# Loads, halves and norm transposes of a two-layer hybrid decoder trunk: second weight rows in halves, a small early read, later transposes

## The chip, the cores and the metric

The kernel runs on one core of a Trainium2 chip. The metric is the device time of one execution in microseconds (us), lower is better. The engines are named as the profile names them: PE (matmuls; PEld its weight loads), DVE (vector), ACT (scalar), POOL (GpSimd) and SP (which here only issues DMAs). A "q" behind an engine's name (SPq, ACTq) marks its sequencer, where DMAs are issued.

## What is computed

Two layers of a decoder trunk on 256 tokens of 1024 values in float32, with three groups of heads side by side, all of 64 wide: 6 stick-breaking heads (`sb`), 6 block-sparse heads with rotary positions (`mb`; with 256 tokens there is one block, so this is causal softmax attention), and 4 heads that attend to 256 memory tokens (`mem`). Cut from the reference:

```python
for layer in range(DEPTH):
    h = rms_norm(x, norm_g[layer])
    proj = jnp.einsum('btd,dc->btc', h, w_in[layer])
    sb_q, sb_k, sb_v, sb_g, mb_q, mb_k, mb_v, mb_g, mem_q, mem_g = jnp.split(proj, split_at, axis=-1)
    o_sb = stick_breaking_attention(sb_q, sb_k, sb_v) * jax.nn.silu(sb_g)
    o_mb = moba_attention(partial_rotary(mb_q), partial_rotary(mb_k), mb_v) * jax.nn.silu(mb_g)
    mk, mv = jnp.split(rms_norm(mem, mem_norm_g[layer]) @ w_mem_kv[layer], 2, axis=-1)
    o_mem = memory_attention(mem_q, mk, mv) * jax.nn.silu(mem_g)
    x = x + jnp.concatenate([o_sb, o_mb, o_mem], axis=-1) @ w_out[layer]
return rms_norm(x, final_norm_g)
```

`w_in` has 3584 columns in each layer, `w_mem_kv` 512 and `w_out` 1024, each over 1024 rows, that is 8 blocks of 128 rows (k = 0 to 7).

## The kernel before, in words

**Weights.** The columns of the weights are cut into pieces (`sb_qk`, `mem_q`, `mb_k` and so on, class `Piece`) whose order in each layer is the table `ORDER`. A piece is cut into chunks of up to 768 columns in all: 768 columns of one block of rows, or 384 of two, or 256 of three. A chunk is read by one DMA into one of 5 buffers `raw` (`dma_chunk`, the DMA itself in the helper `dma`, L332). Then it is split into two parts, hi = the weights cast to fp32r (`hi_task`; `copy`, L266 on DVE, or `act`, L245 on ACT) and lo = raw - hi (`lo_task`, `tt`, L251, DVE), which stand side by side in one of 7 buffers `hl`. The split of a chunk sets its `raw` free, and `lo_task` then issues the next chunk's DMA. A product is made of three matmuls: hi by hi, hi by the activations' lo, and lo by the activations' hi (`mm`, L229). The very first chunk of `sb_qk` (k = 0) is read as two halves of 384 columns; all others come whole.

**Activations.** The first layer's input comes transposed from HBM (`xT`) into the tile `uT`, in blocks of 128 rows: `load_xT`. The norm gain is multiplied in block by block, ACT making the hi part (`scale_hi`, L247) and DVE the lo part (`scale_lo`, L255) of the tile `T`. The first piece runs over k on the outside with six PSUM banks open, so that PE can begin when block 0 of weights and of x is there; for k = 0 it works on the two halves one after the other (`groups` in `main`), for k = 1 to 3 on all six column groups at once, first hi, then lo. At the change of layer `norm_task` multiplies the rows by gain and 1/rms (`stt`, L255, tile `w`, 512 columns at a time), PE transposes four blocks (`tr`, L234), and ACT and DVE copy the bank out as hi and lo into `T`: four such groups, two row halves by two column halves.

**Order of the work.** The program is written out by a scheduler in Python, `Sched`. Every task is a generator that asks for an engine, names what it needs and which buffers it takes, and has a priority; `run` takes the task whose modelled start (`_avail`) is earliest, within a small slack by priority, and `op` adds a modelled cost to the engine's clock. `main` holds the matmuls of the projections, with the lowest priority; scores, sums, turns, norm transposes are tasks of their own and are put between them. What decides is modelled times, so a constant changes the order on all engines. `X67_AT`, `X0_AT`, `X1_AT` and `CST_AT` say behind which chunk's DMA the loads of x blocks 6 and 7, of the rows of x and of the constants are issued; `TRIP_LAT` is the modelled time of a trip through DRAM (`trip`).

In softmax heads (`soft_head`) the four buffers `w` (also used by the norm) are handed out in a fixed order of head pairs: the `mb` pairs first, then the `mem` pairs, by this condition:

```python
first = (2 if mb else 0) if MEM_FIRST[l] else (0 if mb else 3)
_, (w,) = yield R("act", alloc=["w"], cond=lambda: 5 * l + first + h // 2 <= turn["w"] + 1)
```

**Queues at the start.** ACT's queue issues the two halves of k = 0 and then the x block of k = 1; SP's queue issues `gc` (gain columns), x block 0, the chunk of k = 1, x block 2, the chunk of k = 2, x block 3, the chunk of k = 3, and x blocks 4 and 5 together. POOL sets the constant tile `negone` (a memset, L452) and issues one broadcast of the norm's gain row later (`bcast_row`, L447). Score stages and the products with the values work on 64 rows or 64 columns of the PE array (`pair_scores`, `pair_task`), and the scheduler holds them back so as to run them in blocks (`_by_form`).

Of the kernel before, what the change touches and what calls it, by code (L numbers as in the profile page):

```python
# [17 lines left out]
KT = 8  # L18
# [10 lines left out]
KORD = (0, 1, 2, 3, 4, 5, 6, 7)  # L29
LAT_SAME, LAT_CROSS = 130.0, 240.0  # L30
P_H0 = -8
P_RX = 1
# [3 lines left out]
URG = 2  # L36
X67_AT = 6
CST_AT = 7
X0_AT = 9
X1_AT = 12  # L40
DMA_GBS = 380.0
SP_ISSUE = 450.0
DMA_LAT = 2200.0
DMA_GBS_1K = 300.0
TRIP_LAT = 4000.0
MEM_FIRST = (False, False)
MEM_AT = 1
ORDER = (["sb_qk", "mem_q", "mb_k", "mb_q", "mk", "mv", "sb_v", "sb_g", "mb_g", "mb_v", "mem_g"],
         ["mk", "mv", "sb_g", "mb_k", "mb_q", "mb_g", "mem_g", "sb_q", "mem_q", "sb_k", "sb_v", "mb_v"])
GATES = {"sb_g": ((0, 1, 2),), "mb_g": ((0, 1, 2),), "mem_g": ((0,), (1,))}  # L50
HOLD = 4000.0
SPARE2 = 2
DVE_HI = 400.0
# [27 lines left out]
class Sched:  # L81
# [37 lines left out]
    def _avail(self, k, eng):  # L119
        r = k.req  # L120
        t = k.t
# [17 lines left out]
        if cond is not None and not cond():  # L139
            return None  # L140
        return t

# [56 lines left out]
def hybrid_trunk(ctx: ExitStack, tc: tile.TileContext, x, mem, norm_g, w_in, w_mem_kv, w_out,  # L199
# [171 lines left out]
    for p in order:  # L371
        i = 0
        while i < KT:
            kk = [p.kord[i]]
            i += 1
            while i < KT and len(kk) < p.nk and p.kord[i] == kk[-1] + 1:
                kk.append(p.kord[i])
                i += 1
            half = p.width // 2 if not chunks else p.width
            for c in range(0, p.width, half):  # L380
                for n, k in enumerate(kk):
                    p.kmap.setdefault(k, []).append((c, len(chunks), n * half))
                chunks.append((p, kk, c, half))
# [20 lines left out]
    def hi_task():  # L404
        for j, (p, kk, _, w) in enumerate(chunks):
            w = len(kk) * w
            e, _ = yield R(*([] if j == 0 else [("act", 0.833 * w)]), ("dve", 0.52 * w + DVE_HI), 
                           need=[("raw", j)] + ([("free", j - LEAD)] if j >= LEAD else []))
            copy(his[j % LEAD][:, :w], raws[j % RAW][:, :w], e)
            S.mark(("hi", j))  # L410
            prog["hi"] = j + 1
# [18 lines left out]
    def load_xT(k0, k1, q=None, now=0.0):  # L430
        dma(uT[:, k0:k1, :], xT_r[:, k0:k1, :], ("xT", k0), q, now)
        for k in range(k0 + 1, k1):
            S.ready["xT", k] = S.ready["xT", k0]

    dma(gc, gcols, "gc")
    dma_chunk(q=nc.scalar)
    load_xT(0, 1)
    dma_chunk(q=nc.scalar)
    load_xT(1, 2, nc.scalar)
    for k in range(2, 4):  # L440
        dma_chunk()
        load_xT(k, k + 1)
    dma_chunk()
    load_xT(4, 6)

# [124 lines left out]
    def norm_task(l, t, H, done):  # L570
# [3 lines left out]
        for q in range(2):  # L574
            s = slice(q * 512, (q + 1) * 512)
            _, (w,) = yield R("dve", need=[("gb", 0)], alloc=["w"])
            stt(w, src[:, s], r, gb[:, s], OP.mult, OP.mult)
            _, (pt,) = yield R("pe", alloc=["bank"])
            for i in range(4):
# [36 lines left out]
    wTs, scs, sps, ws, Fs, ropes = {}, {}, {}, {}, {}, {}  # L616
    turn = {"sb": 0, "w": 0}
    HCOL = {"sb": 0, "mb": 384, "mem": 768}
# [16 lines left out]
    def pair_scores(l, kind, c):  # L635
# [20 lines left out]
        if kind != "mem":  # L656
            yield R("pe")
            for h in range(2):
                for j, o in enumerate((slice(0, 128), slice(256, 384))):
                    if kind == "sb":  # L660
                        mm(sc[h][:, o], masks[:, 0, :], identb, False, j == 1)
                    else:
                        mm(sc[h][:, o], identb, masks[:, 1, :], False, j == 1)
        for h in range(2):
            S.mark(("qkdone", l, kind, 2 * c + h))
            scs[l, kind, 2 * c + h] = sc[h]
# [42 lines left out]
    def soft_head(l, h, kind):  # L709
        mb = kind == "mb"  # L710
        first = (2 if mb else 0) if MEM_FIRST[l] else (0 if mb else 3)
        reg = [(0, 128), (128, 384)] if mb else [(0, 256), (256, 512)]
        _, (st,) = yield R("dve", alloc=["st"], need=[("qkdone", l, kind, h)])
        sc = scs.pop((l, kind, h))
        for t, (r0, r1) in enumerate(reg):
            nc.vector.tensor_reduce(st[:, t:t + 1], sc[:, r0:r1], axis=AX.X, op=OP.max, negate=True)  # L716
            S.op("dve", 1.0417 * (r1 - r0) + 65.0)
            if t == 0:
                yield R("dve")
        _, (w,) = yield R("act", alloc=["w"], cond=lambda: 5 * l + first + h // 2 <= turn["w"] + 1)  # L720
        for t, (r0, r1) in enumerate(reg):
# [255 lines left out]
    def main():  # L977
# [26 lines left out]
        for l in range(DEPTH):  # L1004
# [45 lines left out]
            if l == 0:  # L1050
# [4 lines left out]
                for k in range(KT):  # L1055
                    if k < 4:
                        groups = [range(3), range(3, 6)] if k == 0 else [range(6)]
                        for g in groups:
# [131 lines left out]
```

## Time and profile before

| | |
|---|---|
| median of 3 runs | 282.25 us (281.93 to 282.3) |
| the profiled execution's own time | 281.82 us |
| its span in the profile | 280.0 us |
| mean granted clock of PE in it | 0.998 of full speed |
| busy: PE, DVE, ACT, POOL | 270.7, 229.9, 185.0, 3.9 us |
| moved by DMA | 60.49 MB, mean 216 GB/s |

The span runs from the first to the last recorded instruction; the execution's own time is 1.8 us longer. Busy times are sums over the engine's instructions, so PE at 97% has some 9 us in which it does nothing; the share says nothing of where these lie. The list of waits of an engine says what ended each stand; the timeline gives start, duration and the stand before it in square brackets.

### The profile page before, as it was taken

To read this page: it belongs to the slowest core of one execution; us is meant where nothing else is said; L and a number is where in the kernel's file an instruction comes from. 1 tells how busy PE (TensorE), PEld (TensorE's weight loads), DVE (VectorE), ACT (ScalarE), POOL (GpSimd) and SP (SyncE) were. 2 spreads that over 40 slices of the span, in tenths; PEclk is the share of its full clock that TensorE was granted. 3 is DMA by queue.
4 is the path that set the end of the run, shared out by engine and by line. 5 is a ranking of instruction groups with operands and counts; after the bars stand their busy time and mean duration, and the time that the engine had idled before them with its cause. 6 is when DMAs were issued, how large, how long until landed. Compare 5 with 4: busy or idle time off the path is not lost.

```text
span 280.0 us, 4979 instructions
## 1 busy us (share of the span) xinstructions
PE 270.7 (97%) x1713; PEld 242.7 (87%) x1713; DVE 229.9 (82%) x514; ACT 185.0 (66%) x414; POOL 3.9 (1%) x10
## 2 busy tenths in 40 slices
PE   7899999999999999999999999999999999999991
PEld 4788999898888898898978899988888898988991
DVE  3789899998999999995889489739999999994273
ACT  3879799984696787771866384648974898433053
POOL 0030000010000000000000000000000000000000
PEclk9999999999999999999999999999999999999999
DMA  6999938697588998885476846857358988890004
GB/s 218 348 385 367 367 103 259 188 246 285 165 267 212 263 314 250 242 210 167 129 248 199 272 147 208 250 167 218 104 148 290 248 265 219 263 248 14 0 0 150
DMA packets 45720, 60.49 MB, mean 216 GB/s; under 512 B 3328, under 2 KB 42368, under 8 KB 45696
## 3 DMA queue, kind: packets, MB, share of 16 engines
q1 hardware_dynamic: 44688, 58.22, 67.7%
q0 software_dynamic: 288, 1.05, 1.5%
q10 hardware_dynamic: 720, 0.92, 1.0%
q8 instruction: 13, 0.21, 0.3%
q14 instruction: 11, 0.09, 0.1%
HBM read 53.89 MB, written 6.29 MB: 215 GB/s over the span
## 4 chain that ended last, share of the span: by engine, by line
PE 91%; DMA 4%; ACT 2%; DVE 2%; issue 1%; ACTq 0%; DVEq 0%
PE bank L229 90%; DMA uT<-xT_dram 2%; DMA raw<-in_w_in_dram 2%; PE bank L234 1%; DVE hl L251 1%; ACT hl L245 1%; DVE xs L251 0%; ACT junk L247 0%; DVE w L255 0%; ACT rn L247 0%; ACT ss L247 0%; ACT T L247 0%; ACT T L245 0%; ACTq L332 0%; ACT L206 0%
## 5 line engine op out<-in xcount | busy, mean ns | idle before, releaser
L251 DVE TENSOR_TENSOR hl<-raw,hl 128x768 fp32r<-128x768 f32 (+2 forms) x111 | 101.2, 919 | 8.8 <-ACT hl L245 7.3
L229 PE MATMUL bank<-T,hl 128*128 128x512 f32 (+1 forms) x582 | 106.6, 340 | 1.6 <-ACT hl L245 1.1
L229 PEld LDWEIGHTS bank<-T,hl 128*128 128x128 f32 x582 | 89.2, 190 | 15.7 <-ACT hl L245 1.3
L245 ACT CAST hl<-raw 128x768 fp32r<-128x768 f32 (+2 forms) x100 | 79.4, 808 | 21.2 <-PE bank L229 16.1
L229 PE MATMUL bank<-hl,T 128*128 128x384 f32 (+1 forms) x448 | 82.0, 337 | 0.0
L229 PEld LDWEIGHTS bank<-hl,T 128*128 128x128 f32 x448 | 76.4, 188 | 1.6 <-issue 0.2
L229 PE MATMUL bank<-hl,mxhi 128*128 128x384 f32 (+1 forms) x192 | 45.3, 319 | 0.0
L229 PEld LDWEIGHTS bank<-hl,mxhi 128*128 128x128 f32 x192 | 33.3, 189 | 1.5 <-issue 1.5
L229 PE MATMUL bank<-hl,mxlo 128*128 128x384 f32 (+1 forms) x96 | 30.4, 317 | 0.0
L247 ACT ACTIVATE junk<-xs 128x384 bf16<-128x384 f32 (+2 forms) x16 | 8.4, 523 | 21.6 <-DVE xs L251 20.8
L247 ACT ACTIVATE w<-bank,st 128x256 f32<-128x256 f32 (+1 forms) x40 | 17.3, 447 | 5.2 <-DVE st L716 4.2
L229 PEld LDWEIGHTS bank<-hl,mxlo 128*128 128x128 f32 x96 | 18.1, 189 | 0.0
L247 ACT ACTIVATE ga<-ga 128x768 f32<-128x768 f32 (+1 forms) x24 | 14.9, 628 | 1.6 <-DVE ga L255 1.3
L247 ACT ACTIVATE T<-uT,gc 128x256 fp32r<-128x256 f32 x24 | 11.2, 500 | 5.2 <-DMA uT<-xT_dram 5.2
L245 ACT COPY gT<-bank 128x256 f32<-128x256 f32 x16 | 5.9, 372 | 12.3 <-PE bank L229 12.2
L251 DVE TENSOR_TENSOR xs<-bank,xs 128x384 f32<-128x384 f32 (+1 forms) x12 | 6.1, 510 | 9.3 <-PE bank L229 9.3
L255 DVE SCALAR_TENSOR_TENSOR T<-uT,gc,T 128x256 fp32r<-128x256 f32 x24 | 11.3, 479 | 2.8 <-ACT T L247 2.8
L251 DVE TENSOR_TENSOR gT<-bank,gT 128x256 f32<-128x256 f32 x16 | 6.7, 418 | 7.9 <-ACT gT L245 7.8
L716 DVE TENSOR_REDUCE st<-bank 128x1 f32<-128x256 f32 (+1 forms) x40 | 13.0, 367 | 0.0
L746 DVE STREAM_TRANSPOSE D<-w 128x384 f32<-128x384 f32 (+1 forms) x20 | 12.2, 617 | 0.0
L247 ACT ACTIVATE a<-a 128x384 f32<-128x384 f32 x24 | 11.9, 529 | 0.0
L259 DVE TENSOR_SCALAR w<-w,st 128x256 f32<-128x256 f32 (+1 forms) x40 | 11.0, 320 | 0.0
(112 smaller groups left out, 251.8 us busy)
## 6 DMA issues: line engine op xcount, KB each, us to landing
raw<-in_w_in_dram SPq DMA_DIRECT2D x71, 384.0 KB, 4.7
raw<-in_w_out_dram SPq DMA_DIRECT2D x20, 384.0 KB, 4.4
raw<-in_w_mem_kv_dram SPq DMA_DIRECT2D x8, 384.0 KB, 3.3
Z<-D SPq DMA_DIRECT2D x8, 384.0 KB, 4.7
T<-Z SPq DMA_DIRECT2D x24, 96.0 KB, 5.1
uT<-memT_dram SPq DMA_DIRECT2D x8, 256.0 KB, 5.5
Z<-D SPq DMA_DIRECT2D x4, 512.0 KB, 5.2
T<-Z SPq DMA_DIRECT2D x16, 128.0 KB, 5.0
```

Of the source, the lines that this page charges most:

```text
L229: nc.tensor.matmul(out, lhsT=lhsT, rhs=rhs, start=start, stop=stop, **kw)
L234: nc.tensor.transpose(out, in_, idt)
L245: nc.scalar.copy(out, in_)
L247: nc.scalar.activation(out, in_, func, **kw)
L251: nc.vector.tensor_tensor(out, a, b, op=op)
L255: nc.vector.scalar_tensor_tensor(out, a, s, b, op0=op0, op1=op1)
L259: nc.vector.tensor_scalar(out, a, s, None, op0=op)
L716: nc.vector.tensor_reduce(st[:, t:t + 1], sc[:, r0:r1], axis=AX.X, op=OP.max, negate=True)
L746: nc.vector.transpose(o, w[:, :n * 128].rearrange("p (m j r) -> p m j r", j=4, r=32))
```

## The change

Five things are done.

1. Chunks 0 to 3 are halves now, so the second rows' weights (k = 1) come as two DMAs of 384 columns too, each with its own hi and lo. `main` works on k = 1 in two groups, as on k = 0. Chunk numbers move up by one, and with them the constants `X67_AT` and `X1_AT`; `X0_AT` goes down. The hi of chunks 0 and 2 (the first halves) may only be made by DVE.
2. The x block of k = 1 is issued by SP, ahead of the two halves of k = 1, and no longer by ACT.
3. Ahead of everything POOL issues a DMA into a new tile `ahead`: 16 values (64 bytes) of the first row of each of the 8 blocks of rows of `w_in` of layer 0. Nothing reads the tile.
4. In `_avail`, all PE tasks outside `main` count as ready 0.1 us later than modelled (`PE_LATE`), norm transposes 1.2 us later (`NORM_LATE`).
5. `ORDER` and `TRIP_LAT` change, and the buffers `w` go to head pairs in the order in which their scores were written (`place`) instead of the order by `MEM_FIRST`.

```diff
--- before.py
+++ after.py
@@ -28,25 +28,26 @@
 RAW = 5
 KORD = (0, 1, 2, 3, 4, 5, 6, 7)
 LAT_SAME, LAT_CROSS = 130.0, 240.0
+PE_LATE = 100.0
+NORM_LATE = 1200.0
 P_H0 = -8
 P_RX = 1
 P_M0 = 12
 P_RM = 12
 P_M1 = 4
 URG = 2
-X67_AT = 6
+X67_AT = 7
 CST_AT = 7
-X0_AT = 9
-X1_AT = 12
+X0_AT = 8
+X1_AT = 13
 DMA_GBS = 380.0
 SP_ISSUE = 450.0
 DMA_LAT = 2200.0
 DMA_GBS_1K = 300.0
-TRIP_LAT = 4000.0
-MEM_FIRST = (False, False)
+TRIP_LAT = 3500.0
 MEM_AT = 1
-ORDER = (["sb_qk", "mem_q", "mb_k", "mb_q", "mk", "mv", "sb_v", "sb_g", "mb_g", "mb_v", "mem_g"],
-         ["mk", "mv", "sb_g", "mb_k", "mb_q", "mb_g", "mem_g", "sb_q", "mem_q", "sb_k", "sb_v", "mb_v"])
+ORDER = (["sb_qk", "mb_k", "mem_q", "mb_q", "mv", "mk", "sb_v", "sb_g", "mb_g", "mb_v", "mem_g"],
+         ["mk", "mv", "mb_k", "mb_g", "mb_q", "mem_g", "sb_q", "mem_q", "sb_k", "sb_g", "sb_v", "mb_v"])
 GATES = {"sb_g": ((0, 1, 2),), "mb_g": ((0, 1, 2),), "mem_g": ((0,), (1,))}
 HOLD = 4000.0
 SPARE2 = 2
@@ -138,7 +139,7 @@
         cond = r.get("cond")
         if cond is not None and not cond():
             return None
-        return t
+        return t + r.get("late", PE_LATE) if eng == "pe" and k.gen.__name__ != "main" else t
 
     def _by_form(self, cands):
 
@@ -376,7 +377,7 @@
             while i < KT and len(kk) < p.nk and p.kord[i] == kk[-1] + 1:
                 kk.append(p.kord[i])
                 i += 1
-            half = p.width // 2 if not chunks else p.width
+            half = p.width // 2 if len(chunks) < 4 else p.width
             for c in range(0, p.width, half):
                 for n, k in enumerate(kk):
                     p.kmap.setdefault(k, []).append((c, len(chunks), n * half))
@@ -404,7 +405,7 @@
     def hi_task():
         for j, (p, kk, _, w) in enumerate(chunks):
             w = len(kk) * w
-            e, _ = yield R(*([] if j == 0 else [("act", 0.833 * w)]), ("dve", 0.52 * w + DVE_HI), 
+            e, _ = yield R(*([] if j in (0, 2) else [("act", 0.833 * w)]), ("dve", 0.52 * w + DVE_HI), 
                            need=[("raw", j)] + ([("free", j - LEAD)] if j >= LEAD else []))
             copy(his[j % LEAD][:, :w], raws[j % RAW][:, :w], e)
             S.mark(("hi", j))
@@ -432,15 +433,18 @@
         for k in range(k0 + 1, k1):
             S.ready["xT", k] = S.ready["xT", k0]
 
+    ahead = sb("ahead", [KT, 16])
+    nc.gpsimd.dma_start(ahead, w_in[0].rearrange("(k p) c -> k p c", p=128)[:, 0, 0:16])
     dma(gc, gcols, "gc")
     dma_chunk(q=nc.scalar)
     load_xT(0, 1)
     dma_chunk(q=nc.scalar)
-    load_xT(1, 2, nc.scalar)
-    for k in range(2, 4):
-        dma_chunk()
-        load_xT(k, k + 1)
+    load_xT(1, 2)
     dma_chunk()
+    dma_chunk()
+    load_xT(2, 3)
+    dma_chunk()
+    load_xT(3, 4)
     load_xT(4, 6)
 
     def bcast_row(vec, name):
@@ -575,7 +579,7 @@
             s = slice(q * 512, (q + 1) * 512)
             _, (w,) = yield R("dve", need=[("gb", 0)], alloc=["w"])
             stt(w, src[:, s], r, gb[:, s], OP.mult, OP.mult)
-            _, (pt,) = yield R("pe", alloc=["bank"])
+            _, (pt,) = yield R("pe", alloc=["bank"], late=NORM_LATE)
             for i in range(4):
                 tr(pt[:, i * 128:(i + 1) * 128], w[:, i * 128:(i + 1) * 128], ident)
             S.free("w", w)
@@ -614,7 +618,7 @@
 
 
     wTs, scs, sps, ws, Fs, ropes = {}, {}, {}, {}, {}, {}
-    turn = {"sb": 0, "w": 0}
+    turn, place = {"sb": 0, "w": 0}, {}
     HCOL = {"sb": 0, "mb": 384, "mem": 768}
     VN = {"sb": "sb_v", "mb": "mb_v", "mem": "mv"}
 
@@ -661,6 +665,8 @@
                         mm(sc[h][:, o], masks[:, 0, :], identb, False, j == 1)
                     else:
                         mm(sc[h][:, o], identb, masks[:, 1, :], False, j == 1)
+        if kind != "sb":
+            place[l, kind, c] = len(place)
         for h in range(2):
             S.mark(("qkdone", l, kind, 2 * c + h))
             scs[l, kind, 2 * c + h] = sc[h]
@@ -708,7 +714,6 @@
 
     def soft_head(l, h, kind):
         mb = kind == "mb"
-        first = (2 if mb else 0) if MEM_FIRST[l] else (0 if mb else 3)
         reg = [(0, 128), (128, 384)] if mb else [(0, 256), (256, 512)]
         _, (st,) = yield R("dve", alloc=["st"], need=[("qkdone", l, kind, h)])
         sc = scs.pop((l, kind, h))
@@ -717,7 +722,7 @@
             S.op("dve", 1.0417 * (r1 - r0) + 65.0)
             if t == 0:
                 yield R("dve")
-        _, (w,) = yield R("act", alloc=["w"], cond=lambda: 5 * l + first + h // 2 <= turn["w"] + 1)
+        _, (w,) = yield R("act", alloc=["w"], cond=lambda: place[l, kind, h // 2] <= turn["w"] + 1)
         for t, (r0, r1) in enumerate(reg):
             act(w[:, r0:r1], sc[:, r0:r1], AF.Exp, bias=st[:, t:t + 1], accum_out=st[:, 2 + t:3 + t])
         S.free("bank", sc)
@@ -1054,7 +1059,7 @@
                     accs.append((yield from bank()))
                 for k in range(KT):
                     if k < 4:
-                        groups = [range(3), range(3, 6)] if k == 0 else [range(6)]
+                        groups = [range(3), range(3, 6)] if k < 2 else [range(6)]
                         for g in groups:
                             j, o = p.loc(k, g[0] * 128)
                             o -= g[0] * 128
```

How the order of instructions moves is shown at two places. The first is the start. ACT's rows before, from its second DMA issue on (`T` is the activations' hi part, `hl` the weights' hi part, `raw` the weights as read, `uT` the x block):

```order
L332 DMA raw_90<-in_w_in_dram 128x384
L332 DMA uT<-xT_dram 128x256
L247 ACTIVATE T_74<-uT,gc 128x256
L245 CAST hl_95<-raw_90 128x384
L247 ACTIVATE T_74<-uT,gc 128x256
L245 CAST hl_96<-raw_91 128x768
L247 ACTIVATE T_74<-uT,gc 128x256
L245 CAST hl_97<-raw_92 128x768
L247 ACTIVATE T_74<-uT,gc 128x256
L245 CAST hl_98<-raw_93 128x768
```

And now:

```order
L333 DMA raw_90<-in_w_in_dram 128x384
L248 ACTIVATE T_74<-uT,gc 128x256
L246 CAST hl_95<-raw_90 128x384
L248 ACTIVATE T_74<-uT,gc 128x256 x2
L246 CAST hl_98<-raw_93 128x768
L248 ACTIVATE T_74<-uT,gc 128x256 x3
L246 CAST hl_99<-raw_89 128x768
L246 CAST hl_100<-raw_90 128x768
L246 CAST hl_94<-raw_91 128x768
```

The DMA of `uT` has gone from ACT; the cast of the weights of k = 1 (`hl_96` before) is no longer on ACT, and three `T` (x blocks 3, 4 and 5) stand in a row ahead of the cast of k = 3's weights, `hl_99` now and `hl_98` before. On SP the rows before were:

```order
L332 DMA gc<-gcols_dram 128x32
L332 DMA uT<-xT_dram 128x256
L332 DMA raw_91<-in_w_in_dram 128x768
L332 DMA uT<-xT_dram 128x256
L332 DMA raw_92<-in_w_in_dram 128x768
L332 DMA uT<-xT_dram 128x256
L332 DMA raw_93<-in_w_in_dram 128x768
L332 DMA uT<-xT_dram 128x2x256
L332 DMA raw_89<-in_w_in_dram 128x768
```

And now:

```order
L333 DMA gc<-gcols_dram 128x32
L333 DMA uT<-xT_dram 128x256 x2
L333 DMA raw_91<-in_w_in_dram 128x384
L333 DMA raw_92<-in_w_in_dram 128x384
L333 DMA uT<-xT_dram 128x256
L333 DMA raw_93<-in_w_in_dram 128x768
L333 DMA uT<-xT_dram 128x256
L333 DMA uT<-xT_dram 128x2x256
L333 DMA raw_89<-in_w_in_dram 128x768
L333 DMA raw_90<-in_w_in_dram 128x768
```

Two `uT` follow `gc`, then the two halves of k = 1, x block 2, the chunk of k = 2 (`raw_93`), x block 3 and x blocks 4 and 5; the chunk of k = 3, which stood ahead of these last as `raw_93`, stands behind them as `raw_89`, the buffer that the first chunk had.

The second place is the change of layer on PE, in the memory's key piece (`mk`), at its second bank; L234 are the transposes of `norm_task`, four to a group, and the group of `w_115` is the second to come. Before:

```order
L229 MATMUL bank_102<-T_74,hl_94 128x512
L229 MATMUL bank_102<-T_74,hl_94 128x256
L229 MATMUL bank_102<-T_74,hl_94 128x512
L229 MATMUL bank_102<-T_74,hl_94 128x256
L234 MATMUL bank_108<-cst,w_115 128x128 x4
L229 MATMUL bank_102<-T_74,hl_94 128x512
L229 MATMUL bank_102<-T_74,hl_94 128x256
L234 MATMUL bank_104<-cst,w_113 128x128 x4
```

And now:

```order
L230 MATMUL bank_105<-T_74,hl_95 128x512
L230 MATMUL bank_105<-T_74,hl_95 128x256
L230 MATMUL bank_105<-T_74,hl_95 128x512
L230 MATMUL bank_105<-T_74,hl_95 128x256
L230 MATMUL bank_105<-T_74,hl_95 128x512
L230 MATMUL bank_105<-T_74,hl_95 128x256
L230 MATMUL bank_105<-T_74,hl_96 128x512
L230 MATMUL bank_105<-T_74,hl_96 128x256
L235 MATMUL bank_102<-cst,w_115 128x128 x4
L230 MATMUL bank_105<-T_74,hl_96 128x512
```

The group of `w_115` stood behind 4 matmuls of this bank, with the next group (`w_113`) 2 matmuls behind it; it stands behind 8 of them now. With the first bank's 16 ahead that is 20 before and 24 now.

## Rows read from the trace of the kernel before

**Rows 1.** the page, part 1: busy us, share of the span and instructions of each engine.

```profile
PE 270.7 (97%) x1713; PEld 242.7 (87%) x1713; DVE 229.9 (82%) x514; ACT 185.0 (66%) x414; POOL 3.9 (1%) x10
```

**Rows 2.** waits of PE: engine, line, waited for: us in total, times, longest.

```profile
PE bank L229 <- ACT hl L245: 1.1, 1, 1.1
PE bank L234 <- DVE w L255: 0.6, 1, 0.6
PE bank L229 <- ACT T L247: 0.4, 1, 0.4
PE bank L229 <- ACT rn L247: 0.2, 1, 0.2
```

**Rows 3.** timeline, first 9 us: start, duration, engine, line, operation, [stand before <-releaser].

```profile
1.68 0.45 ACTq L332 DMA_DIRECT2D uT<-xT_dram  x1
...
3.27 0.36 DVE L266 CAST hl<-raw 128x384 fp32r<-128x384 f32 x1 [2.13 <-DMA raw<-in_w_in_dram]
...
4.16 0.51 ACT L247 ACTIVATE T<-uT,gc 128x256 fp32r<-128x256 f32 x1 [2.15 <-DMA uT<-xT_dram]
...
4.72 2.85 PE L229 MATMUL bank<-T,hl 128*128 128x256 f32 x18 [0.37 <-ACT T L247]
...
7.16 0.38 SPq L332 DMA_DIRECT2D uT<-xT_dram  x1
7.39 0.51 ACT L247 ACTIVATE T<-uT,gc 128x256 fp32r<-128x256 f32 x1 [2.32 <-DMA uT<-xT_dram]
...
7.80 0.81 ACT L245 CAST hl<-raw 128x768 fp32r<-128x768 f32 x1
...
8.67 0.50 PE L229 MATMUL bank<-T,hl 128*128 128x512 f32 x1 [1.10 <-ACT hl L245]
```

**Rows 4.** windows: length, busy us of PE, PEld, DVE, ACT, POOL, PEclk, DMA share, GB/s.

```profile
1.50:5.50 4.00, 3.63 (x10) 1.53 (x9) 1.72 (x4) 1.43 (x3) 0.00 (x0) 1.00 0.82 242
3.00:3.50 0.50, 0.50 (x3) 0.17 (x2) 0.23 (x1) 0.00 (x0) 0.00 (x0) 1.00 1.07 375
3.50:4.00 0.50, 0.50 (x3) 0.00 (x0) 0.47 (x2) 0.00 (x0) 0.00 (x0) 1.00 1.48 255
4.00:4.50 0.50, 0.36 (x1) 0.00 (x0) 0.22 (x1) 0.34 (x1) 0.00 (x0) 1.00 0.40 101
```

**Rows 5.** waits of SP, first 10 us, the longest.

```profile
SPq L332 <- DMA raw<-in_w_in_dram: 2.7, 1, 2.7
```

**Rows 6.** timeline of PE, whole span.

```profile
8.67 16.49 PE L229 MATMUL bank<-T,hl 128*128 128x512 f32 x92 [1.10 <-ACT hl L245]
...
48.85 0.33 PE L229 MATMUL bank<-ah,negT 128*128 128x384 f32 x1
...
66.55 1.48 PE L229 MATMUL bank<-uT 64*128 64x128 f32 x16
67.96 0.62 PE L229 MATMUL bank<-masks,identb 128*128 128x128 bf16 x8
...
72.73 0.93 PE L229 MATMUL bank<-uT 64*128 64x128 f32 x8
73.49 1.56 PE L229 MATMUL bank<-mem_k,mem_q 64*128 64x256 f32 x8
```

**Rows 7.** timeline of POOL, 50 to 160 us.

```profile
59.04 0.73 POOL L447 DMA_DIRECT2D gb<-in_norm_g_dram  x1 [40.92 <-DMA uT<-Z]
```

**Rows 8.** timeline of the change of layer, 143.9 to 145 us.

```profile
144.06 1.41 DVE L255 SCALAR_TENSOR_TENSOR w<-xs,ss,gb 128x512 f32<-128x512 f32 x2
...
144.86 0.33 PE L234 MATMUL bank<-cst,w 128*128 128x128 f32 x1 [0.61 <-DVE w L255]
```

**Rows 9.** the tile `uT`, issues between 7 and 7.3 us.

```profile
DMA to landing us min/median/max: 4.5/4.5/4.5
```

**Rows 10.** windows, 40 to 50 us, columns as above.

```profile
40.00:50.00 10.00, 10.00 (x61) 10.00 (x61) 9.72 (x25) 9.28 (x22) 0.00 (x0) 1.00 0.69 227
```

**Rows 11.** timeline of DVE, 42 to 49 us.

```profile
47.80 0.55 DVE L251 TENSOR_TENSOR al<-a,ah 128x384 fp32r<-128x384 f32 x1
```

## The prediction

> **What bounds the kernel now.** I read the page first: PE is busy for 270.7 of 280.0 us, DVE for 229.9 [rows 1]. A busy PE need not be a useful PE, so the second view is the list of waits of PE: after the warm-up matmuls it waits for anything only four times, 1.1 us for ACT's `hl`, 0.6 us for DVE's `w`, 0.4 us for ACT's first `T` and 0.2 us for ACT's `rn` [rows 2]. That is the whole room for a change that leaves the matmuls as they are, apart from the 4.7 us ahead of the first matmul of weights. Both orders hold 1585 matmuls, so the matmul work itself is taken as unchanged.
>
> The third view is the timeline of the start [rows 3]. PE starts on weight row block 0 at 4.72, ends it at 7.57 and stands until 8.67. Block 1 needed its weights, for whose landing SP stood 2.7 us, until 7.16 [rows 3, 5], and its x columns, issued on ACT's queue at 1.68 and landed just ahead of the `T` that reads them, 7.39 [rows 3]. From that landing on ACT makes `T`, then `hl` (7.80), and PE starts: 1.3 us from landing to matmul. The stretches of the DMA view show why the landings are late: 242 GB/s on the mean from 1.5 to 5.5 us, with 375 GB/s just before a hole of 255 and then 101 GB/s between 3.5 and 4.5 us [rows 4], though transfers of two queues are out by then. The hole lies where the first packets of block 1 would be under way.
>
> **The change part by part.**
>
> *Start.* Block 1's weights come as two halves, its x columns go onto SP's queue ahead of them, and ACT's queue keeps block 0's two halves alone. Ahead of the end of block 1 there now stand gc (16 KB), four halves of 192 KB and two x blocks of 128 KB, 1040 KB or 1.06 MB. At the pace of before, hole and all, 4.0 us x 242 GB/s = 0.97 MB had moved by 5.5 [rows 4], and the remaining 0.10 MB takes 0.3 us more at 375: everything landed by about 6.0, with some receipt time. Without the hole it is 0.5 us sooner: (375-255) and (375-101) over half a microsecond each are 0.20 MB, 0.53 us at 375. The chain behind the landing was 1.3 us with one whole cast; now DVE casts the first half alone, 0.36 us by the half cast of block 0 [rows 3], and PE starts when that half is there. So block 1 is ready between 6.8 and 7.4, and block 0 ends at 7.57 or a tenth sooner: the wait of 1.1 us goes in either case. Bounds: 1.1 gained, or with the hole kept and every step late 0.5. I take **-1.1**.
>
> Behind it the blocks follow at 16.49 us for 92 matmuls [rows 6], 0.18 each, 2.15 us for a block of 12, so block 3 is wanted at 7.6 + 4.3 = 11.9. ACT now makes `T` of blocks 3, 4 and 5 ahead of the cast of block 3's weights, so that cast waits for the transfer of x blocks 4 and 5. In before SP issued that one at 7.16, behind its stand of 2.7 us for the landing of block 1's weights [rows 3, 5]; in the new program its wait is for a transfer two places earlier, that of x block 0, which had landed by 4.16 [rows 3]. Block 3's weights, whose buffer was a fresh one, now come into the first chunk's, which is free soon after its cast of 3.27 [rows 3], long before SP gets there. I take no new wait here and price the other case below.
>
> The touch (eight rows of 64 B on GpSimd's queue) costs POOL an issue; the nearest row is 0.73 us for one of 512 KB [rows 7]. Behind it on POOL stands only a memset of `negone`, which PE reads after all eight blocks of the first piece: nothing. What it does to the DMA engines is the unknown of this change. Gain: the hole of 0.5 us, which the order of transfers hides anyway. Loss: between nothing and the hole once for every block. I take 0. One issue more on SP (two halves) stands where SP no longer waits 2.7 us: nothing. The earlier constants and x rows feed norms that PE's waits do not name [rows 2]: nothing.
>
> *Layer change.* PE's second group of norm transposes waits 0.61 us for `w`; DVE runs the two `w` of this place from 144.06 and PE starts at 144.86 [rows 8]. That group now stands after 24 instead of 20 matmuls of the key piece; four at 0.18 us [rows 6] bring PE there 0.72 us later, with matmuls that it had to do anyway. ACT's and DVE's instructions up to that `w` are the same in kind and order, apart from the first transposes' evacuation, which moves back. The 0.6 goes; bounds 0 (the `w` slips by as much) and 0.6. The third and fourth groups come 12 matmuls, 2.1 us, apart with less DVE work than that between them. I take **-0.6**.
>
> *Middle.* The order of pieces changes (keys of the block heads before the memory queries, values before keys of the memory, the stick-breaking gate of layer 1 late). The 64-row score stages come as nine blocks instead of seven, the 64-column ones as seven instead of eight. Two score pairs in a row took 1.41 us from start to start, 66.55 to 67.96, and one alone 0.76, 72.73 to 73.49 [rows 6]: 0.11 us for a split, **+0.1** for the one block more. The wait of 0.2 for `rn` belongs to a bank that the new order doesn't use there, but another bank is as close: 0 taken, -0.2 to +0.3 as bounds.
>
> Sum: -1.1 - 0.6 + 0.1 = -1.6. The profiled execution took 281.82 us (span 280.0), which makes 280.2; the median of the runs is 282.25, 0.43 more, so the forecast is **280.6**.
>
> **A rule against the touch.** The hole is worth 0.53 us, and the trace does not say whether a small early transfer fills it or only moves it: in it the traffic of the core as a whole sank [rows 4]. The Trainium skill (DMA: Bandwidth & Descriptors, Issuing engines are not separate DMA queues) says that transfers from any issuing engine run on the same 16 DMA engines and interleave there, so that another queue saves issue time alone. By that, the touch has no engine of its own, and a slow read would hold up the packets of block 0 behind it. As a case of this kernel it is rival B.
>
> **The rivals.**
>
> A, the forecast: both waits go, 280.6. Chance 0.51. E, the same and more: a first x landing earlier by up to the 0.4 us that PE waits for `T` [rows 2], and 0.6 in the middle from better places: 279.6. Chance 0.10.
>
> B, the hole moves to block 0: the first matmul starts 0.5 late, so only 0.6 of the 1.1 is kept, 281.1. For it: the hole is at the first read of new rows. Against: only eight small packets do it. 0.11.
>
> C, ACT's order: if x blocks 4 and 5 are issued at 7.16 as in before and land 4.5 us later, as they did there [rows 9], at 11.66, then two `T` of 0.51 and the cast of 0.81 [rows 3] end at 13.5, PE waits 1.6 at block 3 and is 0.5 behind before: +0.5 - 0.6 + 0.1, 282.2. Against: SP's long wait is gone. 0.07.
>
> D, DVE sets the pace from 40 to 60 us, where it is 9.7 of 10 us busy [rows 10]. PE comes to the first suffix sums with 87 instead of 93 natural-form matmuls ahead of them, 1.1 us, and with the start's 1.1 at 46.6 instead of 48.85 [rows 6]; DVE ended their input at 47.80 + 0.55 = 48.35 [rows 11]. If DVE does not move forward, PE waits 1.75, of which 1.1 is matmuls still owed: +0.65 for -1.1, and the whole comes to 282.4. Against: over the span DVE is idle for 50 us [rows 1], and an earlier start moves its work forward too. 0.07.
>
> S, slower: the eight first reads queue on one or two DMA engines, one slow read after the other. Block 0 and its x columns are spread over all engines and land with the last. Each further block costs a hole of 0.53 us: seven more on one engine hold the first matmul by 3.7 us, for a net of +2.1, 284.4; it decides from five in a row on (2.65 - 1.6 = +1.05, 283.3). For it: the hole of before pulled the whole core down to 101 GB/s [rows 4]. Against: eight rows can go to eight engines. 0.14.
>
> **How the numbers follow.** No change means within 0.2%, 0.56 us, of 282.25, about what a measurement of this kernel can tell. A, B and E are faster: 0.72. C and D are within: 0.14. S is slower: 0.14. The range goes from E with the 0.2 of `rn` on top, 279.4, to 282.6, past C and D; it leaves out S and little else.
>
> **What would show it.** Right: PE's list of waits has neither the 1.1 for `hl` nor the 0.6 for `w`; block 1 follows block 0 without a gap at about 7.5 us; the stretch from 3.5 to 4.5 us moves over 300 GB/s; the first matmul of weights still starts at 4.7, give or take 0.3. B and S show as a later first matmul with a late landing of `uT` or the first `raw`; C as a PE wait near 12 us for ACT's `hl`; D as a PE wait for DVE's `al` near 47 us. The reasoning is wrong if the time falls while those two waits stay, or if PE's busy time itself changes by more than half a microsecond.

## The result, and the profile after

The changed kernel takes 279.24 us (median of 4 runs, 278.95 to 279.51), the kernel before 282.27 (4 runs, 281.93 to 282.46): a ratio of 0.990 with a 95% interval of 0.987 to 0.9931, or 3.0 us less. The forecast was 280.6, 1.65 less; it has the sign, and a little over half of the size. The measured median lies 0.16 below the low end of the stated range, less than its own runs lie apart.

The page's first lines of the changed kernel (busy us, share, instructions):

```profile
span 277.7 us, 4991 instructions
...
PE 270.4 (97%) x1713; PEld 242.6 (87%) x1713; DVE 231.0 (83%) x517; ACT 184.9 (67%) x413; POOL 4.2 (2%) x11
```

PE's busy time is 270.4 where it was 270.7 [rows 1]: 2.0 of the span's 2.3 us (280.0 to 277.7) come from stands. The two profiled executions lie 2.3 apart, the medians 3.0, so the waits below need not add up to the 3.0. The list of waits of PE shows it, to be read against [rows 2]:

```profile
PE bank L230 <- DVE junk L985: 1.2, 1, 1.2
PE bank L230 <- DVE dg L256: 0.2, 1, 0.2
PE bank L230 <- ACT T L248: 0.2, 1, 0.2
```

The 1.1 us for `hl` and the 0.6 for `w` are gone, as forecast, the 0.2 for `rn` too; 0.2 of 0.4 is left of the first `T`, and 0.2 is new, for `dg` (the 1/rms of the rows of x, set on a diagonal). The first row is the stand ahead of the warm-up, the same in both. Against [rows 3], the timeline of the start now:

```profile
3.95 0.51 ACT L248 ACTIVATE T<-uT,gc 128x256 fp32r<-128x256 f32 x1 [1.93 <-DMA uT<-xT_dram]
...
4.51 5.80 PE L230 MATMUL bank<-T,hl 128*128 128x256 f32 x33 [0.15 <-ACT T L248]
...
5.25 0.51 ACT L248 ACTIVATE T<-uT,gc 128x256 fp32r<-128x256 f32 x1 [0.35 <-DMA uT<-xT_dram]
...
6.38 0.36 DVE L267 CAST hl<-raw 128x384 fp32r<-128x384 f32 x1
6.97 0.36 DVE L267 CAST hl<-raw 128x384 fp32r<-128x384 f32 x1 [0.23 <-DMA raw<-in_w_in_dram]
```

The first half of block 1's weights was cast from 6.38 and the second from 6.97; PE starts 0.2 sooner and runs past block 0 and block 1 without a stand: 33 matmuls in this window, which ends at 10 us, and the list of waits has none for blocks 1 to 7. The windows of the DMA view beside [rows 4] (length, busy us of PE, PEld, DVE, ACT, POOL, PEclk, DMA share, GB/s):

```profile
1.50:5.50 4.00, 3.85 (x11) 1.75 (x10) 1.92 (x4) 1.72 (x4) 0.62 (x2) 1.00 0.89 267
...
3.50:4.00 0.50, 0.50 (x3) 0.00 (x0) 0.47 (x2) 0.05 (x1) 0.00 (x0) 1.00 0.98 338
4.00:4.50 0.50, 0.36 (x1) 0.00 (x0) 0.32 (x2) 0.50 (x2) 0.00 (x0) 1.00 1.30 341
4.50:5.00 0.50, 0.49 (x2) 0.49 (x3) 0.50 (x2) 0.39 (x1) 0.00 (x0) 1.00 0.84 266
5.00:5.50 0.50, 0.50 (x4) 0.50 (x4) 0.49 (x1) 0.25 (x1) 0.00 (x0) 1.00 1.10 276
```

The hole of 255 and 101 GB/s between 3.5 and 4.5 us is 338 and 341 now; behind it stands a flatter dip of 266 and 276. The mean from 1.5 to 5.5 has gone from 242 to 267. At the change of layer, beside [rows 8]:

```profile
141.87 0.75 DVE L256 SCALAR_TENSOR_TENSOR w<-xs,ss,gb 128x512 f32<-128x512 f32 x1 [1.06 <-ACT ss L248]
...
143.13 0.60 PE L235 MATMUL bank<-cst,w 128*128 128x128 f32 x4
```

The second `w` is ready at 141.87 + 0.75 = 142.62, and PE comes at 143.13.

### The profile page after: what moved, and what is told of

It reads as the page before. It is cut to its first block, busy times and chain, and to the rows that moved or that the text cites. A ratio compares the mean times of both kernels' runs of the same rounds, so it can differ in the third digit from the quotient of the medians.

```text
span 277.7 us, 4991 instructions
## 1 busy us (share of the span) xinstructions
PE 270.4 (97%) x1713; PEld 242.6 (87%) x1713; DVE 231.0 (83%) x517; ACT 184.9 (67%) x413; POOL 4.2 (2%) x11
## 4 chain that ended last, share of the span: by engine, by line
PE 88%; DMA 4%; ACT 3%; DVE 3%; issue 0%; SPq 0%; DVEq 0%; ACTq 0%
PE bank L230 87%; DMA raw<-in_w_in_dram 3%; PE bank L235 1%; DMA uT<-xT_dram 1%; ACT ga L248 1%; ACT a L248 1%; DVE gT L252 0%; DVE ga L256 0%; DVE hl L252 0%; DVE a L256 0%; ACT w L248 0%; ACT hl L246 0%; DVE sb_v L267 0%; DVE D L751 0%; DVE ah L267 0%
## 5 line engine op out<-in xcount | busy, mean ns | idle before, releaser
L246 ACT CAST hl<-raw 128x768 fp32r<-128x768 f32 (+2 forms) x101 | 80.4, 811 | 22.5 <-PE bank L230 9.8
```

The costliest lines, as they stand in the source:

```text
L246: nc.scalar.copy(out, in_)
```

## The experiments

All times are medians; "before" and the ratio with its 95% interval are from the same chip as the kernel. The before of the four groups of runs took 282.27, 282.21, 282.15 and 282.20, so the medians can be set side by side, with some tenths of scatter. The ratio is not the quotient of the two medians and can differ from it (run 12: 0.9962, quotient 0.9951).

**1. The touch taken away.**

```diff
-    ahead = sb("ahead", [KT, 16])
-    nc.gpsimd.dma_start(ahead, w_in[0].rearrange("(k p) c -> k p c", p=128)[:, 0, 0:16])
```

> The changed kernel without the small GpSimd read; every other instruction stands where it did. Theory (halves and order of the loads make the start's gain, the touch nothing): 279.2, within 0.3 of the changed kernel, first matmul of weights at 4.5, no wait for hl at block 1. Rival (the touch fills the hole): 279.8 to 280.3, a hole like the 101 GB/s one back between 3.5 and 5 us, and PE waits 0.5 to 1 for hl or T of block 1. Other rival (the touch costs): 278.7, with the first uT and the first raw landing sooner.

Measured: 279.09 (6 runs), ratio 0.9895 (0.9862 to 0.9928). Against the changed kernel's 279.24 the touch is worth nothing that these runs can tell. In its profiled execution the hole of before has not come back between 3.5 and 4.5 us (windows, columns as above):

```profile
3.50:4.00 0.50, 0.50 (x2) 0.00 (x0) 0.46 (x2) 0.00 (x0) 0.00 (x0) 1.00 1.31 335
4.00:4.50 0.50, 0.35 (x1) 0.00 (x0) 0.46 (x1) 0.25 (x1) 0.00 (x0) 1.00 0.91 328
```

**2. The touch alone**, in the kernel before.

> The kernel before with the small GpSimd read added and nothing else. Theory (touch worth nothing): 282.3, hole and 1.1 us wait for hl as before. Rival (the touch fills the hole): 281.3 to 281.8, the stretch 4.0 to 4.5 over 300 GB/s and the wait for hl 0.6 or less. Other rival (eight first reads in a row hold the DMA engines): 283 or more, first matmul at 5.2 or later.

Measured: 282.45 (12 runs), ratio 1.0003 (0.9979 to 1.0027): nothing again. The hole is still there (windows, columns as above):

```profile
3.50:4.00 0.50, 0.50 (x3) 0.00 (x0) 0.47 (x2) 0.00 (x0) 0.00 (x0) 1.00 1.26 190
4.00:4.50 0.50, 0.36 (x1) 0.00 (x0) 0.27 (x1) 0.20 (x1) 0.00 (x0) 1.00 0.54 139
```

The rows of the tile `ahead` in the changed kernel fit that: issued at 1.2 us, it lands 3.3 us later, at about 4.5, as PE begins block 0.

```profile
L437 POOL DMA_DIRECT2D ahead<-in_w_in_dram x1: 664/664/664, 1.2 to 1.2; - x1
...
DMA to landing us min/median/max: 3.3/3.3/3.3
```

**3. The old start** with the rest of the change: the touch out, and the hunks of `half`, `hi_task`, `groups`, the loads and the `_AT` constants undone.

> The changed kernel with the whole start as before: no touch, the second rows' weights whole, x block 1 on ACT's queue, the old constants for the later loads. What is left of the change is the later norm transposes and the orders. Theory (start worth 1.4 by the milestones of the two traces, the rest 0.9): 280.6, PE waits 1.1 for hl at 7.6 and nothing at the layer change. Rival (a late start is absorbed in the DVE-bound stretch behind it, so that the start gains nothing in the end): 279.2 to 279.6.

Measured: 281.06 (12 runs), ratio 0.9972 (0.9948 to 0.9995). PE's list has the wait for `hl`, 1.4 in this execution, and nothing at the layer change: the theory's place and nearly its size, 1.8 us above the changed kernel.

**4. The new start alone**, those hunks and the touch in the kernel before.

> The kernel before with the new start alone (touch, halves, loads, constants); no later transposes, old orders. Theory: -1.4 of the start kept to the end, 280.9, the wait of 0.6 for w at the layer change still there. Rival (the gain is eaten by the stretch from 30 to 60 us in which DVE is full): 281.8 to 282.3, with a new PE wait for DVE there.

Measured: 281.45 (12 runs, 279.24 to 283.06), ratio 0.9963 (0.9934 to 0.9992). The wait for `hl` is gone, that for `w` is 1.0. No new wait for DVE stands between 30 and 60 us, so the rival has no support; that this start is worth less alone (0.8) than taken out of the changed kernel (1.8) is within the scatter of these runs and not settled.

**5. The norm transposes no later than other tasks**, in the changed kernel.

```diff
-NORM_LATE = 1200.0
+NORM_LATE = 100.0
```

> The changed kernel with the norm transposes no later than other PE tasks (0.1 instead of 1.2 us): they stand as early on PE as in the kernel before. Theory (the later place takes the wait for w): 279.9, PE waits 0.6 to 1.1 for w at about 142 us. Rival (the wait is DVE's place in the layer's end and the orders moved it, the delay does nothing): 279.2, no wait for w.

Measured: 280.83 (12 runs), ratio 0.9952 (0.993 to 0.9975), 1.6 above the changed kernel. The wait is back, 1.04 us, and the timeline of the layer change shows the chain in front of it:

```profile
139.15 0.62 ACT L246 CAST hl<-raw 128x512 fp32r<-128x512 f32 x1 [1.31 <-DMA raw<-in_w_mem_kv_dram]
...
140.10 0.83 ACT L246 CAST hl<-raw 128x768 fp32r<-128x768 f32 x1 [0.33 <-DMA raw<-in_w_in_dram]
140.84 0.41 ACT L248 ACTIVATE junk<-xs 128x256 bf16<-128x256 f32 x1
...
141.57 0.57 ACT L246 CAST T<-bank 128x512 fp32r<-128x512 f32 x1
...
142.18 0.69 DVE L252 TENSOR_TENSOR T<-bank,T 128x512 fp32r<-128x512 f32 x1 [1.68 <-ACT T L246]
...
142.78 1.41 DVE L256 SCALAR_TENSOR_TENSOR w<-xs,ss,gb 128x512 f32<-128x512 f32 x2
...
143.58 0.66 PE L235 MATMUL bank<-cst,w 128*128 128x128 f32 x4 [1.04 <-DVE w L256]
```

In ACT's order the cast of the memory's key weights waits 1.31 us for their landing, the next cast 0.33 for its own; the row statistics (`junk`), the copy of the first transposes (`T`) and, on DVE, its lo part stand behind them, and `w` behind that. In the profiled execution of before the same two casts stood less (timeline of ACT, 138 to 146 us):

```profile
140.57 0.62 ACT L245 CAST hl<-raw 128x512 fp32r<-128x512 f32 x1 [0.69 <-DMA raw<-in_w_mem_kv_dram]
141.71 0.84 ACT L245 CAST hl<-raw 128x768 fp32r<-128x768 f32 x1 [0.52 <-DMA raw<-in_w_in_dram]
```

Their stands add up to 1.21 in before, 1.65 in run 2, 1.56 in run 4 and 1.64 here, and PE's wait for `w` was 0.61, 1.06, 0.98 and 1.04: short where the stands are short. In these four executions the length of this wait goes with when two weight transfers land; no run moved the landings alone.

**6. The old orders**, with the old modelled trip time and the old order of the `w` buffers, the new start and the later PE tasks staying.

```diff
-ORDER = (["sb_qk", "mb_k", "mem_q", "mb_q", "mv", "mk", ...
+ORDER = (["sb_qk", "mem_q", "mb_k", "mb_q", "mk", "mv", ...
-TRIP_LAT = 3500.0
+TRIP_LAT = 4000.0
+MEM_FIRST = (False, False)
```

> The changed kernel with the old orders of pieces, the old modelled trip time and the old order of the w buffers; the new start and the later PE tasks stay. Theory (orders worth nothing, as forecast with +0.1): 279.2, give or take 0.4. Rival (the orders give what the parts of start and later transposes leave open, about 0.5 to 1): 279.8 to 280.3, with waits of PE between 30 and 120 us that the changed kernel doesn't have.

Measured: 285.61 (6 runs), ratio 1.0113 (1.0081 to 1.0146), 6.4 above the changed kernel. Neither expectation held. PE's list has 2.3 us for `mxhi` and 0.6 for `mxlo`, the gated head outputs as hi and lo; the next run has the same two waits and shows where they lie.

**7. The later PE tasks alone**, in the kernel before.

```diff
+PE_LATE = 100.0
+NORM_LATE = 1200.0
...
-        return t
+        return t + r.get("late", PE_LATE) if eng == "pe" and k.gen.__name__ != "main" else t
```

> The kernel before with the later PE tasks alone (0.1 us, norm transposes 1.2): old start, old orders. Theory (wait for w worth 0.6 to 1.1): 281.3 to 281.7, PE's list without the wait for w, the 1.1 for hl still there. Rival (w slips as much as PE does): 282.2, a wait for w of 0.5 or more.

Measured: 287.00 (6 runs), ratio 1.0181 (1.0149 to 1.0213). Neither time was expected. The wait for `w` is gone and that for `hl` is 0.6, but 2.3 and 0.6 us are new at the end of layer 0. PE's timeline there:

```profile
118.63 0.87 PE L231 MATMUL bank<-T,mb_v 128*64 128x256 f32 x8
121.80 0.44 PE L231 MATMUL bank<-hl,mxhi 128*128 128x384 f32 x1 [2.30 <-DVE mxhi L268]
122.87 0.69 PE L231 MATMUL bank<-hl,mxlo 128*128 128x384 f32 x1 [0.62 <-DVE mxlo L253]
```

and in the kernel before at the same place:

```profile
118.51 1.08 PE L229 MATMUL bank<-T,mv 128*64 128x256 f32 x8
119.52 0.44 PE L229 MATMUL bank<-hl,mxhi 128*128 128x384 f32 x1
```

Both have begun the output projection, which takes row blocks 0 to 5 first, when the last product with the values comes. Before, that is a product of the memory heads (`mv`, row blocks 6 and 7), and the matmuls behind it work on blocks 0 to 5. Here it is the last product of the block heads (`mb_v`, block 5), 15 matmuls into the projection, that is behind blocks 0 to 4, and the very next matmul needs its result: gate, `mxhi` and `mxlo`, on a DVE that is also busy with the gates and the memory's `T`. Behind these two stands PE ran at the lower clock, 1.2 GHz (window; PEclk is the third number from the end):

```profile
123.00:126.00 3.00, 3.00 (x10) 3.00 (x11) 3.00 (x8) 0.94 (x3) 0.00 (x0) 0.50 0.16 42
```

The trace's clock record gives the lower clock from 122.7 to 126.1. The stands, 2.9 us, and half of these 3.4 us (an estimate: PE was busy and at half speed) make 4.6 of the 6.2 that this run takes longer than run 12; the rest is not broken down.

**8. x block 0 ahead of the gain columns** on SP's queue, without the touch.

```diff
-    dma(gc, gcols, "gc")
-    dma_chunk(q=nc.scalar)
     load_xT(0, 1)
+    dma(gc, gcols, "gc")
+    dma_chunk(q=nc.scalar)
```

> The changed kernel without the small GpSimd read and with x block 0 issued ahead of the gain columns on SP's queue; nothing else. In the runs so far PE's first matmul of weights waits 0.2 to 0.5 us for T of block 0, whose x block lands last. Theory (x block 0 lands 0.3 to 0.4 sooner and PE starts at 4.36, as the warm-up ends): 278.8. Rival (the gain columns become the last to land, since they are 128-byte rows): 279.2 or more, the same wait for T.

Measured: 280.15 (6 runs), ratio 0.9935 (0.991 to 0.996), 1.1 slower than run 1. The rival: `T` now waits for the gain columns and starts at 4.15. A second thing came with it: the schedule put DVE's cast of block 1's first half, which stood 1.00 for its landing, ahead of the lo part of block 0's second half, and PE waits 0.37 for that one (timeline of the start).

```profile
4.15 0.51 ACT L248 ACTIVATE T<-uT,gc 128x256 fp32r<-128x256 f32 x1 [2.13 <-DMA gc<-gcols_dram]
...
4.71 2.84 PE L230 MATMUL bank<-T,hl 128*128 128x256 f32 x15 [0.35 <-ACT T L248]
...
6.64 0.36 DVE L267 CAST hl<-raw 128x384 fp32r<-128x384 f32 x1 [1.00 <-DMA raw<-in_w_in_dram]
...
7.92 1.91 PE L230 MATMUL bank<-T,hl 128*128 128x256 f32 x10 [0.37 <-DVE hl L252]
```

**9. The second rows' weights whole**, with one cast, which may be on ACT again, and one group of matmuls for block 1; the `_AT` constants go down by one with the chunk numbers. The touch and the order of the loads stay. The main line of the edit:

```diff
-            half = p.width // 2 if len(chunks) < 4 else p.width
+            half = p.width // 2 if not chunks else p.width
```

> The changed kernel with the second rows' weights in one whole transfer and one cast; x block 1 stays on SP's queue ahead of it, the touch stays, the matmuls of block 1 run as one group. Theory of the forecast (the moved x block is enough, the halves only shorten the chain): 279.3, no wait for hl at block 1 or one under 0.2. Rival (the whole cast behind the landing, 0.8 instead of 0.36, opens a gap): 279.7 to 280.1 with a wait for hl of 0.4 to 0.9 near 7.3 us.

Measured: 281.44 (12 runs), ratio 0.9975 (0.996 to 0.9991): 2.2 above the changed kernel, more than even the rival said. The timeline of its start:

```profile
5.70 0.51 ACT L248 ACTIVATE T<-uT,gc 128x256 fp32r<-128x256 f32 x1 [0.75 <-DMA uT<-xT_dram]
...
7.74 0.83 ACT L246 CAST hl<-raw 128x768 fp32r<-128x768 f32 x1 [1.52 <-DMA raw<-in_w_in_dram]
...
8.62 4.70 PE L230 MATMUL bank<-T,hl 128*128 128x512 f32 x25 [1.44 <-ACT hl L246]
```

The wait for `hl` is 1.44; another 0.6 for `rbm`, the 1/rms of the memory's rows, is new in PE's list. The x block is early (`T` at 5.70). The whole transfer, issued at the same 2.11 and behind the same bytes, lands at 7.74; the two halves had landed by 6.38 and 6.97. The other traces agree: with halves behind x block 1 on SP's queue (seven traces) each half landed 3.7 to 4.5 us after its issue, a whole transfer 5.4 to 6.2 after (six traces, five of them with the old start). But a second half also takes an issue of SP's: x block 2, the next load, is issued at 3.06 behind the halves and at 2.58 here. Whether the halves land sooner because they are halves or because the loads behind them come later, no run separates.

**10. x block 1 back on ACT's queue**, the halves kept.

```diff
-    load_xT(1, 2)
+    load_xT(1, 2, nc.scalar)
```

> The changed kernel with x block 1 back on ACT's queue behind the two halves of block 0; the halves of block 1 stay on SP. Theory (x block 1 landed last before because of ACT's queue, so the move makes the gain): a wait for T of block 1 of 0.5 to 1, 280.0. Rival (the halves make the gain, and x block 1 gets its bandwidth anyway): 279.2, no wait.

Measured: 280.06 (6 runs), ratio 0.9931 (0.9914 to 0.9948), 0.8 above the changed kernel. The theory's cost, by another road, as the timeline of its start shows:

```profile
6.90 0.51 ACT L248 ACTIVATE T<-uT,gc 128x256 fp32r<-128x256 f32 x1 [1.95 <-DMA uT<-xT_dram]
...
7.44 0.48 DVE L256 SCALAR_TENSOR_TENSOR T<-uT,gc,T 128x256 fp32r<-128x256 f32 x1 [1.90 <-ACT T L248]
...
7.84 0.62 DVE L267 CAST hl<-raw 128x384 fp32r<-128x384 f32 x2
...
8.34 4.91 PE L230 MATMUL bank<-T,hl 128*128 128x512 f32 x26 [1.17 <-DVE hl L267]
```

x block 1 lands for `T` at 6.90; DVE's lo part of it (7.44) stands ahead of the two half casts (7.84), and PE waits for these.

**11. Eight warm-up matmuls**, without the touch.

```diff
-        for _ in range(7):
+        for _ in range(8):
```

> The changed kernel without the small GpSimd read and with eight warm-up matmuls instead of seven, which end at 4.8 and leave no stand ahead of block 0. In the runs so far the granted clock rose to full between 3.9 and 10.6 us, and every microsecond of half clock there costs PE half a microsecond. Theory (the stand ahead of block 0 sets the late rise): clock at full by 4.6 each time, 278.9, and timed runs within 0.5 of one another. Rival (the rise is where it is by chance): 279.1 to 279.3, with the same scatter.

Measured: 279.31 (6 runs, 278.59 to 279.88), ratio 0.991 (0.9891 to 0.9929). No stand ahead of block 0, but the same time and the same scatter: the rival. In the profiled execution the granted clock rose to full at 5.0 us by the trace's clock record, not by 4.6. PE's timeline:

```profile
1.19 3.59 PE L230 MATMUL bank<-junk 128*128 128x512 bf16 x8 [1.19 <-DVE junk L983]
4.59 17.54 PE L230 MATMUL bank<-T,hl 128*128 128x256 f32 x102
```

**12. The norm transposes alone later**, in the kernel before, with `PE_LATE` at 0: on PE only three groups of transposes change place.

> The kernel before with the norm transposes alone later by 1.2 us in the schedule; on PE nothing but the places of three groups of transposes at the layer change moves. Theory of the forecast (the wait for w goes): 281.2 to 281.6, no wait for w in PE's list. Rival (the late transposes make T late, and the first matmul of h waits instead): 282.2 or more, with a wait for ACT's or DVE's T near 150 us.

Measured: 280.83 (12 runs), ratio 0.9962 (0.9947 to 0.9976): 1.4 us less. No wait for `w` is left (timeline of the layer change):

```profile
142.15 0.83 ACT L247 CAST hl<-raw 128x768 fp32r<-128x768 f32 x1 [0.31 <-DMA raw<-in_w_in_dram]
...
143.99 0.75 DVE L257 SCALAR_TENSOR_TENSOR w<-xs,ss,gb 128x512 f32<-128x512 f32 x1 [1.42 <-ACT ss L249]
...
144.80 0.66 PE L236 MATMUL bank<-cst,w 128*128 128x128 f32 x4
...
145.53 0.68 DVE L253 TENSOR_TENSOR T<-bank,T 128x512 fp32r<-128x512 f32 x1
```

`w` is ready at 143.99 + 0.75 = 144.74, and PE comes at 144.80 with other matmuls done. In before `w` was ready at about 144.06 + 0.75 = 144.81, though the second cast on ACT began 0.44 us sooner there (141.71 for 142.15). There the lo part of the first transposes stood on DVE just ahead of `w`:

```profile
143.46 0.69 DVE L251 TENSOR_TENSOR T<-bank,T 128x512 fp32r<-128x512 f32 x1 [0.99 <-ACT T L245]
```

Here it comes behind, at 145.53, as the first transposes too have moved back. From that cast's start to `w` it is 2.59 us here and 3.10 in before: the later transposes also clear the way of `w` by 0.5 us. The rival's wait for `T` near 150 us did not come.

None of these is faster than the changed kernel beyond the scatter; runs 1 and 11 are as fast as it.

## Why the prediction was half the size

**Start, -1.1.** The place holds, and the size as far as these runs can tell: taken out (run 3) the start is worth 1.8, alone (run 4) 0.8 with an interval from 0.2 to 1.9. One step of the working was wrong, "everything landed by about 6.0". By 5.5 us 4.0 x 267 = 1.07 MB had moved, as many bytes as the working put ahead of the end of block 1. But the second half landed only just before 6.97, when 1.51 MB had moved (5.4 us x 280 GB/s from 1.5 to 6.9): some 0.45 MB issued behind it had moved along. The wait went all the same, with a small margin. The first half was cast by 6.74, some 0.6 ahead of the end of block 0 if that took 2.85 again (an estimate: 4.51 + 2.85 = 7.36). Both edits are needed: without the halves 2.2 is lost (run 9), without the moved x block 0.8 (run 10). The two losses do not add up, as the whole start taken out costs 1.8; the 0.6 for `rbm` is a wait that run 9 alone has.

The 1.1 was also one draw. In five executions with the old start PE's wait for `hl` was 1.42 (run 3), 1.10 (before), 0.62 (run 7), 0.20 (run 2, where those weights also came later) and nothing (run 12). The granted clock rose to full at 3.9, 5.7, 6.6, 10.6 and 8.6 us in them, by the traces' clock records. At the lower clock PE is longer at block 0 and so waits less for weights whose landing does not depend on it.

**The touch, 0.** Right, in both directions (runs 1 and 2). The touch does not make the hole go: run 1 has no touch, no hole at that place and no wait for `hl`. Nor is it shown that the new order of loads does, as the depth differs from execution to execution: the lowest half microsecond from 3.5 to 5.5 us had 101 to 255 GB/s in five traces with the old start (255 in run 3) and 137 to 304 in nine with the new one or a variant of it (266 in the changed kernel, 137 in run 9). Rivals B and S, which rested on the touch, fell with that. The Trainium skill (DMA: Bandwidth & Descriptors, Issuing engines are not separate DMA queues) says that transfers of every issuing engine run on the same 16 DMA engines and interleave there. Runs 1 and 2 agree: a read on GpSimd's queue neither led the others nor held them up (279.09 against 279.24, 282.45 against 282.21). What makes the hole was not tried.

**Layer change, -0.6.** This is the term that was mis-sized. The mechanism is as forecast, PE comes later and `w` does not (run 12), and more. The forecast saw that the evacuation of the first transposes moves back, but not that this brings `w` 0.5 us sooner behind the cast; without that PE, which came 0.06 behind `w` in run 12, would by these numbers still have waited. The term measured 1.4 alone by the medians (1.1 by the ratio, interval 0.7 to 1.5) and 1.6 taken out of the changed kernel (run 5). The 0.61 was read from one execution, and other executions of the same place stood 1.06 (run 2, whose order on PE is that of before), 0.98 (run 4) and 1.04 (run 5). That covers the 1.1 of the ratio; for what the medians have beyond it there is no row.

**Middle, +0.1.** Not isolated. Runs 6 and 7 show that the new orders are no free choice: with the old ones the 0.1 us of `PE_LATE`, which the forecast gave no price at all, makes the end of layer 0 late and costs 6.2 us (run 7 against run 12). In the changed kernel all three products of the block heads stand ahead of the output projection, and no stand follows. Run 3 (later tasks and orders) at 281.06 and run 12 (norm transposes alone) at 280.83 leave 0.2 for orders and `PE_LATE` together, within scatter of the +0.1. New orders without `PE_LATE` were not run.

**Rivals C and D** did not come: no wait for `hl` near 12 us, none for `al` near 47 us, though DVE is 9.9 of 10 us busy from 40 to 50 us. Of E, the first x block gave 0.2 in the profiled execution (first matmul at 4.51 for 4.72), but run 1, whose other instructions are the same, began at 4.81. In five traces with the old start it began at 4.68 to 5.07, in the changed kernel and runs 1, 4, 5, 6, 9 and 10 at 4.51 to 4.81; this does not tell a gain of 0.2 from scatter.

The sum by runs is thus about -0.8 to -1.8 for the start and -1.1 to -1.6 for the transposes, which holds the 3.0.

## What to carry to other kernels

A wait read from one execution is one draw: look at what stands ahead of the producer on its engine, and where a DMA landing is in that chain, price the wait by several executions or by a range. When a consumer can come later at no cost (other matmuls are ready), delay it rather than hurry its producer, and look whether the delay also clears the producer's way; but a delay given to all tasks of a kind can turn the last, needed one late, so look first at which product comes last and who needs it. An early transfer that is needed soon can be worth splitting: here the halves landed sooner than the whole. And every input of that step has to be early, not one of them.

## What the runs showed of the hardware that was not expected

PE's pace at the start differs between executions of the same instructions. The 18 matmuls of block 0 took 2.85 us in the profiled execution of before [rows 3]; in run 2, with the same order on PE, 4.21, and in run 3 2.58. PE's timeline of run 2, from 4 us:

```profile
4.86 4.21 PE L229 MATMUL bank<-T,hl 128*128 128x256 f32 x18 [0.50 <-ACT T L247]
9.27 2.00 PE L229 MATMUL bank<-T,hl 128*128 128x512 f32 x5 [0.20 <-ACT hl L245]
```

and of run 3:

```profile
4.68 2.58 PE L230 MATMUL bank<-T,hl 128*128 128x256 f32 x18 [0.48 <-ACT T L248]
8.68 0.50 PE L230 MATMUL bank<-T,hl 128*128 128x512 f32 x1 [1.42 <-ACT hl L246]
```

4.21 / 18 is 0.23 us for a matmul of 256 columns, 2.58 / 18 is 0.14. This goes with the granted clock: by the traces' clock records it rose from 1.2 to 2.4 GHz at 3.9 us in run 3, ahead of block 0, and at 10.6 in run 2, behind it; in before at 5.7, within it. (PEclk says 1.00 in the windows ahead of that, as it counts nothing before a trace's first record.) The same seven warm-up matmuls stood ahead each time. Block 0 alone took up to 1.6 us longer by this. With the old start most of that is taken out of the wait for block 1, which began at 8.68 in run 3 and at 9.27 in run 2. A part of the scatter of the timed runs (280.4 to 283.7 for before) can be that; the timed runs have no trace to tell. Closing the short stand between warm-up and block 0 (run 11) did not narrow the scatter.
